# Where the first layer's modulation is multiplied: TensorE rows in quarters of the array, or sums on VectorE

## The chip, the cores and the metric

The kernel runs on one core of a Trainium2 chip. The metric is the device time of one execution in microseconds (us), the median of several runs. The engines are TensorE (PE in the profile, its weight loads PEld), VectorE (DVE), ScalarE (ACT), GpSimd (POOL) and SyncE (SP), whose queue issues nearly all transfers here.

## The reference

A trunk of two layers over 512 tokens of 1024 features, all in float32. A vector `c` gives each layer six modulation vectors; here is what matters of the first layer.

```python
c_act = jax.nn.silu(c)
shift1, scale1, gate1, shift2, scale2, gate2 = jnp.split(c_act @ ada_w[l] + ada_b[l], 6, axis=-1)
h = modulate(rms_norm(x, norm1_g[l]), shift1, scale1)          # h * (1 + scale) + shift
mix = s5_mixer(h, ...)                                         # state space per group of 16 channels, then gelu(y) * sigmoid(gelu(y) @ w_glu + b_glu)
x = x + gate1[:, None, :] * mix
h = modulate(rms_norm(x, norm2_g[l]), shift2, scale2)
x = x + gate2[:, None, :] * swiglu(h, ffn_w_gate[l], ffn_w_up[l], ffn_w_down[l])
```

`c_act @ ada_w[0]` is one row times a matrix of 1024 x 6144, 25.2 MB of weights that are read once. The second layer is attention with shared keys and values and a feed-forward of the same kind, and has its own six vectors, besides two for the keys.

## The kernel before

Features lie on the 128 partitions, in eight tiles of 128; `self.mod` holds all modulation vectors as columns, eight for each vector of 1024. The stages follow one another: the mixer (`s5`), its GLU (`glu`), the feed-forward of layer 0 (`ffn`), attention (`mla`), the feed-forward of layer 1. A scheduler orders the instructions of each engine from the order in which the program is written and from its own estimate of when each is ready; `issue_after` holds an instruction behind another one of the same engine. Each engine, and SP's queue, then runs its list in order. Large products take float32 weights as a high and a low part: `wsplit` loads a raw tile of 512 KB on SP (ring of three buffers, tag `raw`), ScalarE rounds it (L790), GpSimd subtracts (L150), and TensorE makes three passes (L801 to L803). In the GLU and the feed-forward, work is due by a clock of the products traced so far (`tick`, `later`, `chain`).

Layer 0's modulation comes in three ways. Shift1 and scale1 are row products (`ada_row`, L380 to L383): the weights stream through TensorE, the stationary operand is `c_act` repeated over all 128 columns, and four PSUM banks (tag `ad`) hold the result on all partitions; VectorE picks each channel with a mask `sel` and a sum (L628, L629). Gate1 is a job of `ada_jobs` in the mixer: SP loads eight blocks of 128 x 1024 (L274), VectorE multiplies each by a scalar for each partition and adds it to `acc` (L282, L284), and the partitions are summed at the end (L292, L296, L318). Shift2 and scale2 are two such jobs, spread over the GLU's products, one step for each 1.5 us of the clock, with the partition sum as products with ones (L305). Gate2 is the first two of 18 jobs of 128 x 512 blocks that are spread over the feed-forward, one of 144 steps for each 1.8 us of the clock; the other sixteen serve keys and layer 1.

In the mixer, `x` is loaded (L392), turned and squared; the sum of squares (L431) gives the norm of each token. The loop over `q` builds the input and output maps on VectorE, GpSimd and TensorE (L579). `sgu` is the input modulation for each group, and `u` the modulated input (L641, L649). `kernels(q)` makes products on TensorE (L612), adds the skip on VectorE (L147), writes to DRAM (`kd`, L618) and reads the windows back (`tt`, L620); `sums` and `states` make the chunk states (L679, L693), `intra` and `inter` the outputs (L721, L732).

The GLU's first half of the tokens ends in a norm (`norm`, L849, L857), whose result the feed-forward's first products need; the second half's products are made meanwhile.

## Time and profile before

| | us |
|---|---|
| median of 3 runs | 1350.58 |
| lowest and highest | 1349.37, 1353.07 |
| span of the profiled execution, first to last instruction | 1353.7 |
| first product of the GLU (L801) | 193.44 |
| first sum for the norm behind the GLU (L849) | 254.93 |
| last step of the modulation on VectorE (L284) | 686.36 |

The only time recorded for the profiled execution is its span. A row of the timeline gives the start in us from the span's start, the duration, the engine, the line, the operation, its output and inputs by name with partitions x elements, and in brackets the idle time before it with what ended it. One float32 product shows as two records on TensorE.

### The profile page before, as it was taken

How to read it: one execution, taken by the hardware profiler on the slowest of the kernel's cores; microseconds unless marked ns; L12 is line 12 of the kernel's file. 1: busy time of each engine (PE TensorE's matmuls, PEld its weight loads, DVE VectorE, ACT ScalarE, POOL GpSimd, SP SyncE). 2: the span in 40 equal slices, each digit the busy share in tenths (PEclk: the TensorE clock that was granted, in tenths of full speed). 3: DMA queues.
4: the chain of work that ended last, by engine and by line, in shares of the span. 5: the costliest groups of instructions: out<-in, count | busy, mean ns of one | idle time of the engine just before them, and what ended most of it. 6: DMA issues, size and time to landing. Idle time of an engine off the chain costs nothing.

```text
span 1353.7 us, 17703 instructions
## 1 busy us (share of the span) xinstructions
PE 1178.7 (87%) x6649; PEld 989.5 (73%) x6649; DVE 861.0 (64%) x1328; ACT 494.9 (37%) x921; POOL 623.8 (46%) x369
## 2 busy tenths in 40 slices
PE   6727669789998899969599788999899999999998
PEld 3416558688776677758499677888898888888888
DVE  8898989978666777766677899895942222221000
ACT  3314363334112121222236786784432222222222
POOL 6984834625333444443372434414724444444445
PEclk8858889789998999979699899999999999999999
DMA  8503977525556666465564011102522333333333
GB/s 206 156 16 59 107 234 222 171 79 158 174 170 191 185 200 190 145 183 167 176 184 130 28 32 47 32 17 75 165 73 84 94 97 97 96 91 94 104 110 110
DMA packets 230293, 167.46 MB, mean 124 GB/s; under 512 B 10000, under 2 KB 204480, under 8 KB 230208
## 3 DMA queue, kind: packets, MB, share of 16 engines
q1 hardware_dynamic: 229888, 166.31, 43.6%
q8 instruction: 52, 0.85, 0.3%
q14 instruction: 33, 0.27, 0.1%
q10 hardware_dynamic: 320, 0.02, 0.0%
HBM read 163.23 MB, written 3.08 MB: 123 GB/s over the span
## 4 chain that ended last, share of the span: by engine, by line
PE 42%; DVE 32%; DMA 17%; ACT 4%; issue 4%; SPq 0%; POOL 0%; ACTq 0%; DVEq 0%; POOLq 0%
PE ps L801 12%; PE ps L802 12%; PE ps L803 12%; DMA a<-in_ada_w 10%; DVE a L284 9%; DMA a<-in_kv_ada_w 4%; DVE a L144 3%; DVE sums L147 2%; DVE a L809 2%; DVE a L282 2%; DVE a L150 2%; DMA a<-in_x 1%; PE ad L382 1%; PE ps L132 1%; DVE xT L881 1%
## 5 line engine op out<-in xcount | busy, mean ns | idle before, releaser
L150 POOL TENSOR_TENSOR wl<-raw,wh 128x1024 fp32r<-128x1024 f32 (+1 forms) x179 | 435.0, 2438 | 542.9 <-ACT wh L790 497.4
L803 PE MATMUL ps<-a,wl 128*128 128x512 f32 (+1 forms) x1406 | 502.9, 359 | 18.5 <-POOL wl L150 18.5
L801 PE MATMUL ps<-a,wh 128*128 128x512 f32 (+1 forms) x1406 | 499.2, 359 | 12.9 <-DMA a<-in_ada_w 6.0
L802 PE MATMUL ps<-a,wh 128*128 128x512 f32 (+1 forms) x1406 | 501.0, 358 | 9.7 <-DVE a L809 5.3
L803 PEld LDWEIGHTS ps<-a,wl 128*128 128x128 f32 x1406 | 271.4, 194 | 64.4 <-POOL wl L150 24.3
L801 PEld LDWEIGHTS ps<-a,wh 128*128 128x128 f32 x1406 | 269.0, 193 | 55.9 <-ACT wh L790 7.0
L802 PEld LDWEIGHTS ps<-a,wh 128*128 128x128 f32 x1406 | 271.2, 193 | 51.2 <-DVE a L809 5.8
L790 ACT CAST wh<-raw 128x1024 fp32r<-128x1024 f32 (+1 forms) x179 | 181.5, 1018 | 337.4 <-PE ps L802 173.6
L284 DVE SCALAR_TENSOR_TENSOR a<-a,csil,a 128x512 f32<-128x512 f32 (+1 forms) x140 | 186.7, 1334 | 99.5 <-DMA a<-in_ada_w 71.2
L999 DVE TENSOR_TENSOR si<-si,ps 128x512 f32<-128x512 f32 x44 | 30.1, 684 | 154.2 <-PE ps L803 143.2
L808 ACT CAST a<-si 128x512 fp32r<-128x512 f32 x44 | 27.3, 621 | 204.8 <-DVE si L999 204.8
L881 DVE SCALAR_TENSOR_TENSOR xT<-ps,mod,xT 128x256 f32<-128x256 f32 (+1 forms) x35 | 20.2, 577 | 128.1 <-PE ps L803 128.1
L809 DVE TENSOR_TENSOR a<-si,a 128x512 fp32r<-128x512 f32 x44 | 70.7, 1609 | 21.5 <-ACT a L808 21.5
L132 PE MATMUL ps<-ident,a 128*128 128x128 f32 (+1 forms) x304 | 45.1, 288 | 20.6 <-DVE a L1338 6.2
L132 PEld LDWEIGHTS ps<-ident,a 128*128 128x128 f32 (+1 forms) x304 | 36.3, 141 | 27.1 <-issue 6.6
L147 DVE TENSOR_TENSOR sums<-sums,sq 128x256 f32<-128x256 f32 (+1 forms) x36 | 43.9, 1219 | 12.0 <-ACT sq L834 11.5
L834 ACT ACTIVATE sq<-xT 128x256 f32<-128x256 f32 (+1 forms) x36 | 16.3, 452 | 74.5 <-DVE xT L881 71.2
L144 POOL TENSOR_TENSOR ro<-a,rt 128x256 f32<-128x256 f32 (+2 forms) x24 | 13.6, 589 | 60.2 <-ACT a L1351 45.3
L579 PE MATMUL ps<-ident,a 128*128 128x128 f32 x64 | 12.9, 355 | 32.1 <-DVE a L150 32.1
L1412 ACT ACTIVATE a<-ps,mn 128x128 f32<-128x128 f32 (+1 forms) x64 | 34.4, 546 | 16.0 <-DVE mn L1411 15.9
L382 PE MATMUL ad<-adaw,csil 128*128 128x512 f32 x64 | 36.9, 717 | 0.9 <-DMA adaw<-in_ada_w 0.9
L802 PE MATMUL ps<-a,a 128*128 128x256 f32 (+2 forms) x108 | 34.9, 324 | 3.1 <-DVE a L809 3.1
(314 smaller groups left out, 1730.8 us busy)
## 6 DMA issues: line engine op xcount, KB each, us to landing
a<-in_ada_w SPq DMA_DIRECT2D x112, 256.0 KB, 2.9
raw<-in_ffn_w_gate SPq DMA_DIRECT2D x44, 512.0 KB, 4.1
raw<-in_ffn_w_up SPq DMA_DIRECT2D x44, 512.0 KB, 3.9
raw<-in_ffn_w_down SPq DMA_DIRECT2D x42, 512.0 KB, 4.0
adaw<-in_ada_w SPq DMA_DIRECT2D x24, 512.0 KB, 4.6
a<-in_ada_w SPq DMA_DIRECT2D x16, 512.0 KB, 4.8
a<-in_kv_ada_w SPq DMA_DIRECT2D x32, 256.0 KB, 3.5
raw<-in_ffn_w_down SPq DMA_DIRECT2D x21, 384.0 KB, 3.8
```

The lines of the kernel that those rows point to most:

```text
L132: self.nc.tensor.transpose(out=out, in_=in_, identity=ident)
L144: return eng.tensor_tensor(out=out, in0=a, in1=b, op=ALU.mult)
L147: eng.tensor_tensor(out=out, in0=a, in1=b, op=ALU.add)
L150: eng.tensor_tensor(out=out, in0=a, in1=b, op=ALU.subtract)
L284: v.scalar_tensor_tensor(out=acc, in0=x, scalar=self.csil[:, k:k + 1], in1=acc, op0=ALU.mult, op1=ALU.add)
L382: nc.tensor.matmul(pr[i * 2 + h], lhsT=self.csil[:, k:k + 1].to_broadcast([P, P]), rhs=w[:, h * 512:(h + 1) * 512], start=(k == 0), stop=( ...
L790: nc.scalar.copy(out=flat(wh), in_=flat(raw))
L801: mm(out, lhsT=lhs[0], rhs=rhs[0], start=start, stop=False)
L802: mm(out, lhsT=lhs[0], rhs=rhs[1], start=False, stop=False)
L803: self.last_mm = mm(out, lhsT=lhs[1], rhs=rhs[0], start=False, stop=stop).ins
L809: self.nc.vector.tensor_tensor(out=lo, in0=src, in1=hi.bitcast(F32), op=ALU.subtract)
L1412: nc.scalar.activation(out=p[:, self.OFF[t]:self.OFF[t] + w], in_=pt, func=AF.Exp, scale=-1.0, bias=mn[:, t:t + 1], accum_out=su[:, t:t + 1])
```

## The change

All six vectors of layer 0 become row products on TensorE inside the mixer. A step of the new `ada_rows` takes two of the eight row blocks: two loads of 512 KB, then four products of 512 columns. Each has `c_act` over 32 columns only and writes one quarter of the partitions of a single PSUM bank (`ac`): two quarters for each row block, one for each half of its columns. After four such pairs a closing step copies the bank to SBUF on ScalarE and adds the quarters in pairs while it turns the row to columns (four products with `self.rows`); VectorE adds the bias. There are four buffers: three of the ring `raw` and one of its own. The steps (six times four pairs and a closing) are placed by hand: five before the loop over `q`, one in each of its eight turns, five behind `states(0)`, five behind `kernels(3)`, two behind each `inter(q)`. `vectors` moves ahead of them. `sgu` is now made from columns of `self.mod` by products with a mask `spread`. The VectorE jobs for gate1, shift2, scale2 and gate2 go, with the tail for `direct`; PSUM gives one bank of `ad` to `ac`, and `intra` runs three instead of four ahead.

```diff
@@ -68,17 +67,17 @@
         self.psum = None
-        self.banks(ps=2, pb=2, ad=4)
+        self.banks(ps=2, pb=2, ad=3, ac=1)
         self.xT = self.const.tile([P, KT, S], F32, tag="xT", name="xT")
@@ -234,8 +233,11 @@
+        self.rows = self.cst([P, 2], name="rows")
+        nc.vector.tensor_tensor(out=self.rows, in0=self.ident[:, 0:64:32], in1=self.ident[:, 64:128:32], op=ALU.add)
     def vectors(self, pool):
@@ -258,14 +260,45 @@
-    def ada_jobs(self, jobs, w, new, ahead=3, direct=False):
+    def ada_rows(self, jobs, pool):
+        nc, v = self.nc, self.nc.vector
+        def pair(src, col0, i):
+            if i == 0:
+                self.rows_acc = self.ps("ac")
+            ks = (2 * i, 2 * i + 1)
+            ws = [self.ring.tile([P, 1024], F32, tag="raw", name=self.name("adaw"), bufs=3) if k % 4 < 3 else
+                  pool.tile([P, 1024], F32, tag="adaw", name=self.name("adaw")) for k in ks]
+            for k, w in zip(ks, ws):
+                nc.sync.dma_start(out=w, in_=src[k * P:(k + 1) * P, col0:col0 + 1024])
+            for j in range(4):
+                nc.tensor.matmul(self.rows_acc[32 * j:32 * j + 32], lhsT=self.csil[:, ks[j // 2]:ks[j // 2] + 1].to_broadcast([P, 32]),
+                                 rhs=ws[j // 2][:, j % 2 * 512:j % 2 * 512 + 512], start=(i == 0), stop=(i == 3))
+        def close(at):
+            row = self.tmp.tile([P, 512], F32, tag="t1", name=self.name("adrow"))
+            nc.scalar.copy(out=row, in_=self.rows_acc)
+            pt = self.ps()[:, 0:8]
+            for m in range(4):
+                nc.tensor.matmul(pt[:, 2 * m:2 * m + 2], lhsT=row[:, m * P:(m + 1) * P], rhs=self.rows, start=True, stop=True)
+            cols = lambda t: t[:, at:at + 8].rearrange("a (h m) -> a m h", h=2)
+            v.tensor_tensor(out=cols(self.mod), in0=pt.rearrange("a (m h) -> a m h", h=2), in1=cols(self.adab), op=ALU.add)
+        for src, col0, at in jobs:
+            for i in range(4):
+                yield lambda src=src, col0=col0, i=i: pair(src, col0, i)
+            yield lambda at=at: close(at)
+    def ada_jobs(self, jobs, w, new, ahead=3):
...
-        def end(at, acc):
-            pt = self.ps("st")[:, 0:8]
-            with self.tc.issue_after(self.last_mm):
-                for m in range(8):
-                    nc.tensor.matmul(pt[:, m:m + 1], lhsT=acc[:, m * P:(m + 1) * P], rhs=self.ones[:, 0:1], start=True, stop=True)
-            self.add(v, self.mod[:, at:at + 8], pt, self.adab[:, at:at + 8])
         def flush():
-            while whole:
-                end(*whole.pop(0))
             if not ends:
@@ -372,28 +393,17 @@
-            pr = [self.ps("ad") for _ in range(4)]
-            def ada_row(k, i):
-                w = self.ring.tile([P, 1024], F32, tag="raw", name=self.name("adaw"), bufs=3)
-                load = nc.sync.dma_start(out=w, in_=io["ada_w"][0, k * P:(k + 1) * P, i * 1024:(i + 1) * 1024])
-                for h in range(2):
-                    nc.tensor.matmul(pr[i * 2 + h], lhsT=self.csil[:, k:k + 1].to_broadcast([P, P]), rhs=w[:, h * 512:(h + 1) * 512],
-                                     start=(k == 0), stop=(k == KT - 1))
-                return load
-            for n in range(3):
-                ada_row(n // 2, n % 2)
             xj = self.at(X0, [P, 8, 512])
...
                 nc.sync.dma_start(out=xj[h * 64:(h + 1) * 64], in_=xv[h])
-                ada_row((3 + h) // 2, (3 + h) % 2)
             craw = self.at(V0, [P, 2, 2, 4, 64])
...
                 nc.sync.dma_start(out=craw[:, i], in_=io[key].rearrange("o (b t a) p n -> (o a p) b t n", b=2, t=4))
+            self.vectors(sp)
+            ada = self.ada_rows(ada, sp)
+            step = lambda n=1: [f() for f in itertools.islice(ada, n)]
             v.tensor_copy(out=lam[64:96].rearrange("a (b n) -> a b n", b=2),
@@ -521,29 +531,13 @@
             self.add(v, b_s, b_r, b_i)
-            self.acc = sp.tile([P, 1024], F32, tag="acc", name="acc")
...
-            sel = sp.tile([P, 16], F32, tag="sel", name="sel")
-            nc.vector.tensor_reduce(out=sel, in_=self.ident.rearrange("a (r p) -> a p r", p=16), axis=AX.X, op=ALU.add)
             bd = [self.at(M0 + 4 * i, [P, 32, 32]) for i in range(2)]
@@ -554,9 +548,8 @@
             self.mul(g, dsk, dcol.unsqueeze(2).to_broadcast([32, 32, 16]), eye.unsqueeze(1).to_broadcast([32, 32, 16]))
-            for n in range(5, 12):
-                ada_row(n // 2, n % 2)
+            step(5)
             ww = [self.at(W0 + 8 * q, [P, 2, 8, P]) for q in range(4)]
@@ -580,8 +573,7 @@
                 with tc.issue_after(done.ins):
-                    if q % 2 == 0:
-                        row = ada_row(6 + q // 4, q // 2 % 2)
+                    step()
                 with tc.issue_after(copied.ins):
@@ -620,19 +612,20 @@
+            spread = self.at(U0, [P, 8, 8, 16])
+            nc.scalar.copy(out=spread, in_=self.ident.rearrange("a (l p) -> a l p", p=16).unsqueeze(2).to_broadcast([P, 8, 8, 16]))
+            mc = sp.tile([P, 2, 8], F32, tag="mc", name="mc")
+            v.tensor_copy(out=mc[:, 0], in_=self.mod[:, 0:8])
+            v.scalar_tensor_tensor(out=mc[:, 1], in0=self.mod[:, 8:16], scalar=1.0, in1=self.n1g[:, 0:8], op0=ALU.add, op1=ALU.mult)
+            px = self.ps()
+            for l in range(8):
+                nc.tensor.matmul(px[:, l * 16:(l + 1) * 16], lhsT=spread[:, l].rearrange("a r p -> a (r p)"),
+                                 rhs=mc.rearrange("a s f -> a (s f)"), start=True, stop=True)
             sgu = sp.tile([P, 2, 32, 2], F32, tag="sgu", name="sgu")
             for i in range(2):
-                for h in range(2):
-                    big = self.at(U0 + 8 + h * 2, [P, 32, 16])
-                    self.mul(v, big, pr[2 * i + h].rearrange("a (g p) -> a g p", p=16), sel.unsqueeze(1).to_broadcast([P, 32, 16]))
-                    v.tensor_reduce(out=sgu[:, i, :, h], in_=big, axis=AX.X, op=ALU.add)
-            f3 = lambda t: t.rearrange("a g b -> a (g b)")
-            self.add(v, f3(sgu[:, 0]), f3(sgu[:, 0]), f3(vec[:, 0]))
-            self.add(v, f3(sgu[:, 1]), f3(sgu[:, 1]), f3(vec[:, 1]))
-            v.scalar_tensor_tensor(out=f3(sgu[:, 1]), in0=f3(sgu[:, 1]), scalar=1.0, in1=f3(vec[:, 2]), op0=ALU.add, op1=ALU.mult)
-            for _ in range(3):
-                next(ada)()
+                v.tensor_copy(out=sgu[:, i].rearrange("a (f l) b -> a l b f", l=8),
+                              in_=px[:, 0:P].rearrange("a (l s b f) -> a l s b f", l=8, s=2, b=2)[:, :, i])
             kernels(0)
@@ -752,36 +745,29 @@
             states(0)
-            gate = sums(2)
+            step(5)
+            sums(2)
             kernels(2)
...
             kernels(3)
-            with tc.issue_after(row.ins):
-                self.vectors(sp)
-            with tc.issue_after(gate.ins):
-                for _ in range(EARLY):
-                    next(ada)()
+            step(5)
             intra(2)
-            intra(3)
             for q in range(8):
                 inter(q)
-                if q < 4:
-                    intra(q + 4)
+                if q < 5:
+                    intra(q + 3)
                 if q in (1, 3):
                     states(q // 2 + 2)
-                if q == 3:
-                    with tc.issue_after(self.s5_last.ins):
-                        for _ in range(KT - EARLY):
-                            next(ada)()
+                step(2)
+            step(99)
             self.dump("u", u)
...
             self.dump("gel", gel)
-            return next(ada)
     def wsplit(self, shape, src, dst=None):
@@ -919,7 +905,7 @@
-    def glu(self, between, extra):
+    def glu(self, between):
...
-        rest = self.spread_out(extra, 0.5, 1.5, lambda: (self.last_raw,))
-        def after(h):
-            if h == 0:
-                rest()
-            between(h)
...
-        self.outputs(blocks, lambda k: (hi[k], lo[k]), done, 6, after)
+        self.outputs(blocks, lambda k: (hi[k], lo[k]), done, 6, between)
@@ -1455,21 +1434,18 @@
         a0, a1, kv = io["ada_w"][0], io["ada_w"][1], io["kv_ada_w"]
-        first, then = [(a0, 16 * P, 16, 8)], [(a0, at * P, at, 8) for at in (24, 32)]
-        later = [(a0, at * P, at, 4) for at in (40, 44)] + [(kv, 4 * i * P, 96 + 4 * i, 4) for i in range(4)]
+        first = [(a0, at * P, at) for at in (0, 8, 16, 24, 32, 40)]
+        later = [(kv, 4 * i * P, 96 + 4 * i, 4) for i in range(4)]
         later += [(a1, 4 * i * P, 48 + 4 * i, 4) for i in range(12)]
-        end = self.s5(self.ada_jobs(first, lambda n: self.ring.tile([P, n * P], F32, tag="raw", name=self.name("adaw"), bufs=3),
-                              lambda n: self.acc))
+        self.s5(first)
         self.banks(ps=6, st=2)
         self.wring = self.ctx.enter_context(self.tc.tile_pool(name="wring", bufs=4, reuse_waits="tile"))
-        buf, acc = itertools.cycle((80, 84, 88)), itertools.cycle((92, 76))
-        end()
-        self.glu(self.ffn_in(0), self.ada_jobs(then, lambda n: self.at(next(buf), [P, n * P]), lambda n: self.at(next(acc), [P, n * P]), direct=True))
+        self.glu(self.ffn_in(0))
         self.dump("x1", self.xT)
```

## Rows read from the trace of the kernel before

**Rows 1.** The page's chain that ended last: shares of the span by engine.
```profile
PE 42%; DVE 32%; DMA 17%; ACT 4%; issue 4%; SPq 0%; POOL 0%; ACTq 0%; DVEq 0%; POOLq 0%
```

**Rows 2.** Busy time by stretch: us, busy by engine, granted clock, transfers' share, GB/s.
```profile
0.00:49.00 49.00, 36.61 (x153) 21.04 (x153) 40.06 (x135) 16.90 (x46) 35.71 (x76) 0.93 0.79 208
...
109.00:153.00 44.00, 32.45 (x444) 29.72 (x446) 40.10 (x43) 18.18 (x48) 31.21 (x18) 0.84 0.59 77
153.00:193.00 40.00, 27.84 (x250) 25.06 (x245) 33.45 (x39) 18.45 (x37) 18.27 (x9) 0.87 0.79 163
193.00:255.00 62.00, 49.84 (x313) 45.31 (x312) 59.78 (x53) 25.06 (x42) 34.32 (x13) 0.85 0.76 231
...
315.00:432.00 117.00, 109.23 (x460) 85.26 (x459) 80.92 (x108) 24.28 (x32) 44.10 (x17) 0.96 0.59 176
432.00:570.00 138.00, 126.47 (x538) 97.36 (x537) 100.03 (x97) 32.22 (x44) 55.77 (x21) 0.96 0.62 187
570.00:687.00 117.00, 89.13 (x438) 73.12 (x437) 80.06 (x74) 26.39 (x34) 46.67 (x21) 0.85 0.59 174
```

**Rows 3.** The chain in order of time, 0 to 260 us: start, us, what.
```profile
7.17 16.39 DMA a<-in_x
...
254.93 0.87 PE st L849 x4
```

**Rows 4.** VectorE's waits, 0 to 108 us: us in total, times, longest.
```profile
DVE var L210 <- PE ps L431: 6.2, 1, 6.2
```

**Rows 5.** Timeline of the mixer: start us, us, instruction.
```profile
73.17 13.78 DVE L144 TENSOR_TENSOR a<-a,pw 128x512 f32<-128x512 f32 x1
74.17 9.79 POOL L150 TENSOR_TENSOR a<-a 128x512 f32<-128x512 f32 x8
...
100.80 0.68 DVE L144 TENSOR_TENSOR a<-ad,sel 128x512 f32<-128x512 f32 x1
...
108.48 0.22 DVE L633 SCALAR_TENSOR_TENSOR sgu<-sgu,vec 128x64 f32<-128x64 f32 x1
```

**Rows 6.** Timeline of the mixer, weight loads of row, half and whole-array products.
```profile
15.41 0.19 PEld L382 LDWEIGHTS ad<-adaw,csil 128*128 128x128 f32 x1 [0.24 <-issue]
15.84 0.19 PEld L382 LDWEIGHTS ad<-adaw,csil 128*128 128x128 f32 x1 [0.24 <-issue]
...
165.33 0.85 PEld L721 LDWEIGHTS ad<-a,a 128*64 128x64 f32 x16 [0.17 <-issue]
...
178.31 3.07 PEld L732 LDWEIGHTS ad<-a,a 128*128 128x128 f32 x26
```

**Rows 7.** Transfers by line: count, KB of one, median us from issue to landing.
```profile
adaw<-in_ada_w SPq DMA_DIRECT2D x24, 512.0 KB, 4.6
...
kd<-a SPq DMA_DIRECT2D x4, 240.0 KB, 7.8
```

**Rows 8.** Waits of SP's own queue, 100 to 200 us.
```profile
SPq L618 <- DVE a L147: 28.1, 4, 12.9
```

**Rows 9.** VectorE's waits, 108 to 193 us.
```profile
DVE acc L284 <- DMA adaw<-in_ada_w: 6.1, 1, 6.1
```

**Rows 10.** Groups by line, 193 to 255 us: busy us, mean ns; idle before.
```profile
L150 POOL TENSOR_TENSOR wl<-raw,wh 128x1024 fp32r<-128x1024 f32 x11 | 30.7, 2796 | 23.0 <-ACT wh L790 20.1 <-PE st L305 2.9
L284 DVE SCALAR_TENSOR_TENSOR a<-a,csil,a 128x1024 f32<-128x1024 f32 x14 | 26.1, 1866 | 0.9 <-DMA a<-in_ada_w 0.8
L801 PE MATMUL ps<-a,wh 128*128 128x256 f32 x73 | 22.0, 301 | 1.4 <-ACT wh L790 1.4
...
L802 PE MATMUL ps<-a,a 128*128 128x512 f32 x16 | 7.5, 468 | 3.1 <-DVE a L809 3.1
```

**Rows 11.** Timeline of the feed-forward, the first and last of a run of products.
```profile
400.04 0.39 PE L801 MATMUL ps<-a,wh 128*128 128x512 f32 x1
...
406.11 0.39 PE L803 MATMUL ps<-a,wl 128*128 128x512 f32 x1
```

**Rows 12.** TensorE's waits, 305 to 700 us.
```profile
PE st L318 <- DVE part L296: 16.5, 1, 16.5
```

More of the change, by code (lines that the diff above doesn't have):

```diff
@@ L40 @@
 ARENA = 128
-EARLY = 4
 class Scratch:
@@ L259, in vectors @@
         self.kvag, self.qg = cols[:, 48:50], cols[:, 50:52]
-    def ada_jobs(self, jobs, w, new, ahead=3, direct=False):
+    def ada_rows(self, jobs, pool):
[24 more added lines that the diff above has]
+    def ada_jobs(self, jobs, w, new, ahead=3):
         nc, v = self.nc, self.nc.vector
         loads = [(src[k * P:(k + 1) * P, col0:col0 + n * P], n) for src, col0, at, n in jobs for k in range(KT)]
-        tiles, ends, whole = [], [], []
+        tiles, ends = [], []
         def load():
@@ L285, in product @@
             load()
-            if k == KT - 1 and direct:
-                whole.append((at, acc))
-                self.later(3.0, flush)
-            elif k == KT - 1:
+            if k == KT - 1:
                 for a in range(0, n, 4):
```

12 lines of the change are left out of this document (removed).

## The prediction

> **What bounds the kernel now.** I read the page first: of the span, 1353.7 us, TensorE has the largest share of the chain that ended last (42%), VectorE follows with 32%, and waiting for transfers is 17% [rows 1]. That is a mean over stages with different limits, so the second view is the busy time by stage [rows 2]. The reader is to see three kinds of stage there. In the mixer (up to about 193 us) VectorE is busy 40.1 of 44 and 33.5 of 40 us. In the GLU (193 to 255 us) VectorE is busy 59.8 of 62 us while TensorE has idle time. In the first feed-forward TensorE leads, but not fully: 109.2 of 117, 126.5 of 138 and 89.1 of 117 us. After 687 us no instruction of layer 0's modulation is left. So only these three stages can change, and each is costed by what ends its waits last.
>
> **The change part by part.**
>
> *Start of the mixer, up to its input modulation.* Four row loads of 512 KB stand before the end of x's two loads on SP's queue, and x ends a wait of 16.39 us on the chain [rows 3]. VectorE sits idle 6.2 us for the sum of squares of x (L431) [rows 4]. The change puts the row loads behind x: 2.1 MB less ahead of it, at 208 GB/s [rows 2] 10 us of transfer. So that idle gap closes: 6.2 us. The eight small loads of `vectors` move here too, behind x on the same queue; nothing early needs them. The extraction of shift and scale takes VectorE from 100.80 to 108.70 us [rows 5], 7.9 us; its replacement is one ScalarE copy of 128x1024 (twice the 0.68 us of the 128x512 row: 1.4), eight products of 16 columns (at most sixteen records of 0.118 us [rows 6], 1.9; I take 1.0) and two copies to 128x64 (0.22 us each [rows 5]), an estimate of 3 us. That gives 4.9 us, together 11.1. I take 9, because this stretch is also ruled by collisions of VectorE and GpSimd: one 128x512 multiply took 13.78 us while GpSimd did eight subtractions [rows 5], and another order of the same work can collide worse. Ends: 3 and 14.
>
> *The row products themselves.* Before, a product of 512 columns is two records, 0.43 us apart [rows 6]; a pair of loads would be four products, eight records, 3.44 us one after another. In the new form each product fills 32 columns of the array and writes 32 partitions of one PSUM bank. The nearest rows are products that fill halves: their weight loads are 0.85/16 = 0.053 us apart, against 3.07/26 = 0.118 us for whole-array products of as many columns [rows 6]. Halves of one bank thus overlap fully. For quarters the bounds are 3.44 us (no overlap) and 0.86 us (four at once); I take 1.0 us, near the row of the halves. At the change of form stands an idle time of 0.17 us [rows 6], two for each pair, so a pair costs TensorE 1.34 us; 24 pairs cost 32 us. Before the second half of the mixer they fall in a stretch where TensorE waits for VectorE. In 109 to 193 us TensorE idles 44 - 32.5 + 40 - 27.8 = 23.7 us [rows 2], and the eleven pairs that are traced from there on need 14.7. Without that idle time they would cost those 14.7 us. The six closings (a ScalarE copy of 128x512, four small products, an addition) lie on ScalarE's idle time, which is busy 18.2 of 44 and 18.5 of 40 us [rows 2]; uncovered, at 0.68 us a copy, they would cost 4 us. The one accumulator bank makes the next job's first pair wait for the copy, which the loads ahead of it hide.
> The Trainium skill (TensorEngine Tiling (Array Packing), Tiling Modes, Key Properties) says that a change of tiling mode drains the engine. It gives no figure; the idle time just named is what the trace has for it, and without it eleven pairs would need 11 us instead of 14.7, which leaves the sum as it is.
>
> *Second half of the mixer.* Removed: eight VectorE steps of 128x1024 and their tail, and VectorE's wait of 6.1 us for such a load [rows 9]. With five steps behind that wait, at 1.87 us as in the GLU [rows 10], that would be 15 us if VectorE alone set this stretch. But the end hangs on the chain kernels, write to DRAM, read back, products inside a chunk, and on this chain SP waits 28.1 us for VectorE's addition [rows 8], and the write takes 7.8 us to land [rows 7]. Moved here: the loads of 16 steps of 512 KB from the GLU and 16 of 256 KB from the feed-forward, 12.6 MB, all on SP's queue, some of them now ahead of or behind those DRAM round trips, and ahead of the first GLU weights, which use the same three buffers. The mixer's 24 row loads become 48. About 18 of them are left for this stretch after those already in flight, ten more than the eight before. Where transfers were dense they moved 208 GB/s at 0.79 and 231 GB/s at 0.76 of the engines' time [rows 2], 263 to 304 at full share, so 512 KB take 1.7 to 2.0 us and ten such loads 17 to 20 us, where transfers idle 44 x 0.41 + 40 x 0.21 = 26 us [rows 2]. They barely fit. TensorE takes its queue in order: where a pair's load is late, state sums and output products queue behind it, VectorE waits for those, and GpSimd for VectorE. I take a loss of 3 us; ends: a loss of 18 (the ten loads unhidden, at the middle price) and a gain of 15.
>
> *GLU.* Sixteen steps leave VectorE: 14 of L284 alone are 26.1 us busy [rows 10] of its 59.8, and two first ones (L282) go as well, besides 16 matmuls for the partition sums. The norm of the first token half, whose first products (L849) run at 254.93 us [rows 3], no longer waits for VectorE. What is late next? TensorE has run 218 records of 256 columns and 48 of 512 by then; at 0.117 and 0.2335 us (26 records in 6.07 us [rows 11], half of it for half the columns) that is 36.7 us, of which about 9 (some 75 records of 256 columns) belong to the second half already. GpSimd's weight splits take 2.8 us each [rows 10], eight of them 22 us. So the norm could start at about 193 + 28 us, and with an allowance of 10 us for the split of the first inputs and the last tile's additions at 231 us instead of 254.9: 23 us at most (an estimate). Some of that is given back: the products of the second half still have to run behind it, and each needs a GpSimd split that blocks VectorE's additions. I take 18; ends 9 and 23.
> The Trainium skill (SBUF — State Buffer, Who interferes with whom) says that a VectorE instruction with two SBUF inputs and a GpSimd one that reads SBUF exclude each other for a whole instruction. The 13.78 us row agrees. By that rule the VectorE instructions that stay are still blocked, which is the third rival below.
>
> *First feed-forward.* Its chain of steps loses the first 16 of 144 (gate2). Between 315 and 687 us TensorE is idle 7.8 + 11.5 + 27.9 = 47.2 us [rows 2], in part a single wait of 16.5 us for the last steps [rows 12]. Per step that is 0.33 us, so 16 steps are 5.2 us; I take 6. Ends: 2 (the waits are those for weight splits) and 14 (nearly the whole late wait goes).
>
> **Sum.** 9 - 3 + 18 + 6 = 30 us off the profiled span: 1353.7 - 30 = 1323.7. The profiled execution's span is 3.1 us over the median of the runs shown, 1350.58, so I forecast 1321 us (1320.6).
>
> **The rivals.**
> *Slower: row loads hold TensorE in the second half of the mixer.* A row load takes 4.6 us to land [rows 7]. If SP issues each of the eleven pairs only when TensorE already waits, because SP itself sits behind a DRAM round trip [rows 8], the exposed time is 11 x 4.6 = 50.6 us. Against the other gains, 9 + 18 + 6 = 33, the kernel is 17.6 us slower: 1368 us. It decides from 3 us exposed per pair on. For it: one queue, in order, with 28.1 us of blocked issue. Against: four buffers, so two pairs are fetched ahead. 0.10; a milder form that gives back just the gains and ends near 1350: 0.05.
> *Quarters do not overlap.* Then the change does not do what it says: a pair is 3.44 + 0.34 = 3.78 us, eleven are 42 us, 18 over the idle time, and the time is 1339 us. The halves speak against it. 0.10.
> The Trainium skill (TensorEngine Tiling (Array Packing), Gotcha 1: PSUM Pressure) says that row tiles can't use one PSUM bank at once; carried over to these column quarters, which share a bank, it gives this rival. The halves [rows 6] also share one bank and overlap, so the trace speaks against that reading.
> *GpSimd's splits become the GLU's limit.* With 2.8 us per split, and VectorE's additions blocked behind them, the GLU gains 7 instead of 18: 1332 us. For it: GpSimd is busy 34.3 of those 62 us already. 0.12.
> *The second half of the mixer gains.* If the loads fit, VectorE's 6.1 us wait and its steps give 10 there instead of costing 3: 1308 us. 0.18.
>
> **How the numbers follow.** The forecast has 0.40, with its own range 1311 to 1332; gains beyond all of these have 0.05. A measurement of this kernel tells changes from about 0.3% on, 4 us. Faster: 0.40 + 0.10 + 0.12 + 0.18 + 0.05 = 0.85; within: 0.05; slower: 0.10. The range 1302 to 1345 holds the forecast and the last three rivals, 0.80.
>
> **What would show it.** Right: the first product of the GLU lies within some 15 us of 193 us; no VectorE instruction with the modulation's weights lies before the feed-forward; the four weight loads of a pair start well under 0.43 us apart; L849's first products come some 20 us earlier relative to the GLU's start; the feed-forward's steps number 128. Wrong: TensorE shows long waits for `adaw` or `raw` loads between its state sums, or SP a larger wait at the DRAM round trip; or VectorE is as busy in the GLU as before, behind GpSimd. What would make the prediction wrong altogether is a mixer that ends over 30 us later.

## The result, and the profile after

The changed kernel takes 1336.54 us (median; 1332.93 to 1340.58), the kernel before 1349.97 on the same chip: ratio 0.9888, 95% interval 0.9855 to 0.9921. It is faster by 13.4 us. The profiled executions differ by 17.3 us (1353.7 and 1336.4). The table cuts both traces at the same marks: the end of the copy or addition that completes `sgu`, SP's issue of the fourth kernel write (`kd`), the first product of the GLU, the first products of the two norms behind it, and the last residual addition of the first feed-forward. Gains are taken before rounding.

| stretch of the profiled execution, us | before | after | gained | predicted |
|---|---|---|---|---|
| start to `sgu` | 108.7 | 101.8 | 6.9 | 9 (3 to 14) |
| `sgu` to the fourth kernel write | 44.7 | 73.1 | -28.4 | -3 (-18 to 15) for this and the next |
| fourth kernel write to the GLU's first product | 40.0 | 40.2 | -0.2 | |
| GLU's first product to the norm of the first half | 61.4 | 43.0 | 18.3 | 18 (9 to 23) |
| norm of the first half to that of the second | 34.7 | 38.1 | -3.4 | 6 (2 to 14) for this and the next |
| to the last residual of the feed-forward | 436.5 | 415.9 | 20.6 | |
| the rest | 627.7 | 624.2 | 3.5 | 0 |

The busy times by stretch, as in [rows 2], of the changed kernel; the fourth row is the GLU's stretch by its own marks, and the second fence has the same stretch of the kernel before:

```profile
0.00:49.00 49.00, 21.61 (x143) 12.54 (x143) 24.89 (x119) 16.57 (x44) 15.80 (x49) 0.97 0.74 196
109.00:153.00 44.00, 28.28 (x355) 21.42 (x353) 36.42 (x39) 11.86 (x28) 41.44 (x25) 0.84 0.55 122
153.00:193.00 40.00, 27.86 (x248) 21.99 (x244) 24.71 (x23) 13.70 (x24) 20.53 (x12) 0.87 1.01 176
215.16:258.19 43.03, 37.63 (x254) 34.71 (x254) 30.84 (x26) 23.53 (x37) 32.75 (x14) 0.96 0.53 154
570.00:687.00 117.00, 107.12 (x569) 91.47 (x570) 68.91 (x67) 34.09 (x46) 63.76 (x28) 0.94 0.58 171
```

```profile
193.44:254.79 61.35, 49.19 (x310) 44.69 (x308) 59.34 (x52) 24.41 (x41) 33.88 (x13) 0.85 0.76 231
```

In the GLU's stretch VectorE was busy 59.3 of 61.4 us and is busy 30.8 of 43.0; TensorE was busy 49.2 of 61.4 and is busy 37.6 of 43.0, now the largest share. VectorE no longer sets this stretch, as predicted. From 570 to 687 us TensorE is busy 107.1 us against 89.1. The rows of the mixer tell the other story. In the first 49 us GpSimd is busy 15.8 us instead of 35.7, VectorE 24.9 instead of 40.1; GpSimd's work turns up after 109 us (41.4 instead of 31.2). From 153 to 193 us transfers are busy all the time.

Why the start is empty, from TensorE's and GpSimd's timelines of the changed kernel (start, us, instruction, in brackets the idle time before it and what ended it), and in the third fence the same two instructions before:

```profile
20.71 0.35 PE L255 MATMUL ps<-ident,rows_a 52*128 52x52 f32 x1 [18.16 <-DMA rows_b<-in_ada_b]
20.99 0.42 PE L410 MATMUL ps<-ident,a 96*128 96x96 f32 x1
```
```profile
30.29 0.24 POOL L143 TENSOR_TENSOR r<-a 128x32 f32<-128x32 f32 x1 [26.82 <-DVE a L146]
```
```profile
3.91 0.42 PE L400 MATMUL ps<-ident,a 96*128 96x96 f32 x1 [1.32 <-DVE a L397]
12.30 0.24 POOL L144 TENSOR_TENSOR r<-a 128x32 f32<-128x32 f32 x1 [8.87 <-DVE a L147]
```

The transpose L255 belongs to `vectors`. It stands ahead of the transpose of the state matrix (L410; L400 before), which ran at 3.9 us before, and waits 18.2 us for the small loads, which stand behind x on SP's queue. VectorE's discretisation waits for L410, and GpSimd, which takes it up, starts at 30.3 us instead of 12.3.

SP's queue in the second half (start, us of issue, what, how many):

```profile
97.90 8.09 SPq L275 DMA_DIRECT2D adaw<-in_ada_w  x4
128.49 0.34 SPq L610 DMA_DIRECT2D kd<-a  x1
131.03 4.03 SPq L612 DMA_DIRECT2D tt<-kd  x8
...
174.93 0.30 SPq L610 DMA_DIRECT2D kd<-a  x1
...
177.57 3.74 SPq L612 DMA_DIRECT2D a<-kd  x8
181.43 23.38 SPq L275 DMA_DIRECT2D adaw<-in_ada_w  x11
208.56 4.22 SPq L774 DMA_DIRECT2D raw<-in_s_w_glu  x3
```

Between 106 and 128 us SP issues nothing: it waits for the addition that completes the first kernel (22.5 us), and the row loads behind the write wait with it. The fourth write comes at 174.9 us. Then eleven row loads take 23.4 us, 2.1 us each, and only behind them come the GLU's weights. TensorE, which takes its queue in order too:

```profile
129.73 1.87 PE L285 MATMUL ps<-rows,adrow 128*128 128x2 f32 x8 [11.68 <-ACT adrow L282]
...
161.32 1.98 PE L714 MATMUL ad<-a,a 128*64 128x128 f32 x16 [7.31 <-DMA adaw<-in_ada_w]
...
193.57 1.05 PE L277 MATMUL ac<-adaw,csil 128*32 128x512 f32 x4
...
196.09 1.05 PE L277 MATMUL ac<-adaw,csil 128*32 128x512 f32 x4
...
211.32 1.06 PE L277 MATMUL ac<-adaw,csil 128*32 128x512 f32 x8
...
215.16 0.47 PE L787 MATMUL ps<-a,a 128*128 128x512 f32 x1 [0.36 <-DVE mod L287]
```

It stands 11.7 us for the closing's copy on ScalarE, which is queued behind work that waits for VectorE, and 7.3 us for a row load ahead of products (L714) that need none. The rows of L277 are row products. A pair has eight records (four products of two records each), as in the row at 211.32 us: 1.06 us. The two rows of four records are half pairs, the products of one load. Each half took 1.05 us too, so a pair whose loads come apart, as most of these late ones do, takes TensorE about twice the time.

### The profile page after: what moved, and what is told of

It is laid out like the page before. It is cut to its first block, busy times and chain, and to the rows that moved or that the text cites. A ratio compares the mean times of both kernels' runs of the same rounds, so it can differ in the third digit from the quotient of the medians.

```text
span 1336.4 us, 17897 instructions
## 1 busy us (share of the span) xinstructions
PE 1173.5 (88%) x6790; PEld 987.6 (74%) x6790; DVE 781.0 (58%) x1275; ACT 498.3 (37%) x924; POOL 624.8 (47%) x369
## 4 chain that ended last, share of the span: by engine, by line
PE 47%; DVE 27%; DMA 16%; ACT 4%; issue 3%; SPq 2%; POOL 0%; DVEq 0%; ACTq 0%; POOLq 0%
PE ps L788 12%; PE ps L787 12%; PE ps L789 12%; DMA a<-in_ada_w 8%; DVE a L317 6%; DMA a<-in_kv_ada_w 3%; DVE sums L146 3%; DVE a L795 2%; DVE a L143 2%; DMA adaw<-in_ada_w 2%; DVE a L149 2%; PE ps L131 1%; PE ac L277 1%; PE ad L725 1%; DVE a L861 1%
## 5 line engine op out<-in xcount | busy, mean ns | idle before, releaser
L789 PE MATMUL ps<-a,wl 128*128 128x512 f32 (+1 forms) x1406 | 498.5, 356 | 17.2 <-POOL wl L149 17.2
L787 PE MATMUL ps<-a,wh 128*128 128x512 f32 (+1 forms) x1406 | 494.3, 355 | 12.3 <-ACT wh L776 9.6
L787 PEld LDWEIGHTS ps<-a,wh 128*128 128x128 f32 x1406 | 269.9, 194 | 49.7 <-ACT wh L776 11.7
L776 ACT CAST wh<-raw 128x1024 fp32r<-128x1024 f32 (+1 forms) x179 | 181.8, 1018 | 322.7 <-PE ps L788 174.8
L317 DVE SCALAR_TENSOR_TENSOR a<-a,csil,a 128x512 f32<-128x512 f32 x112 | 139.1, 1242 | 91.2 <-DMA a<-in_ada_w 68.2
L795 DVE TENSOR_TENSOR a<-si,a 128x512 fp32r<-128x512 f32 x44 | 77.1, 1754 | 21.6 <-ACT a L794 21.6
L146 DVE TENSOR_TENSOR sums<-sums,sq 128x256 f32<-128x256 f32 (+1 forms) x36 | 51.6, 1434 | 14.5 <-ACT sq L820 14.1
L277 PE MATMUL ac<-adaw,csil 128*32 128x512 f32 x192 | 40.9, 737 | 5.2 <-DMA adaw<-in_ada_w 5.2
L149 POOL TENSOR_TENSOR a<-raw,a 128x1024 fp32r<-128x1024 f32 (+1 forms) x8 | 19.1, 2399 | 56.0 <-DMA raw<-in_s_w_glu 40.0
L572 PE MATMUL ps<-ident,a 128*128 128x128 f32 x64 | 13.4, 355 | 27.0 <-DVE a L149 22.1
L572 PEld LDWEIGHTS ps<-ident,a 128*128 128x128 f32 x64 | 9.4, 182 | 37.1 <-issue 20.0
```

Source lines behind the costliest of these rows:

```text
L146: eng.tensor_tensor(out=out, in0=a, in1=b, op=ALU.add)
L149: eng.tensor_tensor(out=out, in0=a, in1=b, op=ALU.subtract)
L277: nc.tensor.matmul(self.rows_acc[32 * j:32 * j + 32], lhsT=self.csil[:, ks[j // 2]:ks[j // 2] + 1].to_broadcast([P, 32]), rhs=ws[j // 2][: ...
L317: v.scalar_tensor_tensor(out=acc, in0=x, scalar=self.csil[:, k:k + 1], in1=acc, op0=ALU.mult, op1=ALU.add)
L776: nc.scalar.copy(out=flat(wh), in_=flat(raw))
L787: mm(out, lhsT=lhs[0], rhs=rhs[0], start=start, stop=False)
```

## The experiments

Every ratio is to runs of the kernel before on the same chip; as its median was between 1349.07 and 1356.21 us from one group of runs to the next, the ratios are compared, not the times. All marks are from the profiled executions, in us. "Late vectors" is the kernel of experiment 1, and "early" is the loop over `q`. Experiments 2, 4, 8 and the first of 9 leave part of the modulation out and set `self.mod` to zero with one instruction on GpSimd, which the cuts below leave out.

| kernel | ratio (95%) | `sgu` | 1st write | 4th write | GLU's first product | first norm |
|---|---|---|---|---|---|---|
| before | 1 | 108.7 | 117.2 | 153.4 | 193.4 | 254.8 |
| changed | 0.9888 (0.9855, 0.9921) | 101.8 | 128.5 | 174.9 | 215.2 | 258.2 |
| late vectors | 0.9811 (0.9776, 0.9845) | 87.6 | 115.0 | 161.8 | 203.7 | 248.4 |
| changed, two jobs | 0.9705 (0.9660, 0.9750) | 98.0 | 123.4 | 167.0 | 192.9 | 234.2 |
| changed, no loads | 0.9748 (0.9711, 0.9786) | 100.3 | 126.0 | 169.8 | 199.3 | 242.9 |
| before, no gate | 0.9861 (0.9828, 0.9894) | 108.0 | 116.5 | 152.7 | 192.0 | 252.2 |
| late vectors, maps first | 0.9815 (0.9785, 0.9845) | 89.7 | 119.8 | 156.4 | 205.8 | 251.9 |
| late vectors, 12 steps early | 0.9671 (0.9631, 0.9711) | 85.0 | 101.4 | 149.7 | 185.5 | 230.8 |
| changed, one group | 0.9925 (0.9898, 0.9953) | 105.9 | 112.8 | 145.2 | 223.3 | 264.1 |
| late vectors, 16 steps early | 0.9612 (0.9572, 0.9651) | 92.3 | 100.0 | 139.8 | 181.8 | 225.4 |
| before, no late steps | 0.9802 (0.9765, 0.9838) | 107.7 | 116.2 | 152.4 | 195.6 | 237.9 |
| late vectors, two jobs | 0.9560 (0.9527, 0.9593) | 86.1 | 110.1 | 152.5 | 176.0 | 217.7 |
| 16 steps early, two jobs first | 0.9753 (0.9721, 0.9784) | 115.9 | 112.0 | 151.2 | 194.7 | 238.4 |
| late vectors, kernel first | 0.9733 (0.9695, 0.9772) | 83.0 | 97.5 | 133.0 | 197.1 | 241.8 |

**1. Late vectors.**

```diff
-            self.vectors(sp)                    # right behind x
...
+            self.vectors(sp)
             step(5)
```

> The changed kernel, with the small vector loads and their two transposes put behind the discretisation instead of right behind x. Three theories for the mixer's second half, which took 114 us from the modulation's copy (sgu) to the GLU's first product, against 85 us before. A, late start: TensorE's 18.2 us wait for the small loads (rows_b) at the start delays the discretisation, with it GpSimd's output maps (GpSimd starts at 30.3 us instead of 12.3), and these delay the first kernel write (128.5 us instead of 117.2) and all behind it; then this kernel gets back the start and most of the second half: GLU's first product at 190 to 200 us instead of 215, time 1313 to 1322. B, row loads: SP's queue and the transfers of the moved rows set the second half; then the start is won and mostly lost again there: first product at 207 to 215, time 1329 to 1337. C, TensorE and ScalarE: the row products and their closings set it; the same as B here.

The transpose of the state matrix is back at 3.9 us, GpSimd starts at 12.3, `sgu` is complete at 87.6. SP issues the small loads as early as in the changed kernel (9.97 to 19.5 us); what has moved is their transposes on TensorE. So the place of these transposes had cost 14 us at the start. But the first write comes 27 us behind `sgu`, as in the changed kernel, and the GLU starts at 203.7, between what A and B expected; the ratio (0.981, 1323.52 us) is between them too. Late vectors are a part of the loss, not its whole.

**2. Changed, two jobs.**

```diff
-        first = [(a0, at * P, at) for at in (0, 8, 16, 24, 32, 40)]
+        first = [(a0, at * P, at) for at in (0, 8)]
```

> The changed kernel with only the first two jobs (shift and scale of the mixer) multiplied; the other four jobs (32 row loads, their products and closings) are left out, their modulation is zero. A, late start: the second half keeps most of its length, over 100 us from sgu to the GLU's first product, and the time stays above 1322. B or C (the moved work itself): that stretch falls back to 85 to 90 us and the time to 1307 to 1313. The difference to the changed kernel is the whole price of the moved rows in the second half.

From `sgu` to the GLU 94.9 us instead of 113.3: the moved rows cost 18.5 us there, 4.1 of them ahead of the fourth write and 14.4 behind it. Yet `sgu` to the fourth write stays 69.0 us, where the kernel before needs 44.7. Most of the 28.4 us lost in that part does not come from the row work. The time, 1310.95, is what B and C expected; the first part is what A expected, so neither is enough.

**3. Changed, no loads.** For the last four jobs:

```diff
-            for k, w in zip(ks, ws):
-                nc.sync.dma_start(out=w, in_=src[...])
+            if col0 < 2048:                     # as before
+                ...
+            else:
+                ws = [self.xT[:, 0:2].rearrange("a k s -> a (k s)")] * 2
```

> The changed kernel with the row loads of the last four jobs left out: their products read tiles that lie on the chip already, so products, closings and additions stay and 16.8 MB of transfers go; the modulation is wrong. B, row loads: most of the loss goes, sgu to the GLU's first product 85 to 95 us, time 1307 to 1316. C, products and closings: it stays above 105 us, time above 1328. A: above 100 us, time above 1322.

99.0 us from `sgu` to the GLU: of the 18.5 us, 14.3 are the loads' and 4.2 the products' and closings'. C falls as the main cause; B holds for the tail (29.5 us instead of 40.2 behind the fourth write), not ahead of it (69.5).

**4. Before, no gate.**

```diff
-        later = [(a0, at * P, at, 4) for at in (40, 44)] + [(kv, ...
+        later = [(kv, ...
```

> The kernel before, with the first 16 of the 144 steps in the first feed-forward (the gate of that layer) left out; that gate is zero. The prediction gave these steps 6 us (0.33 us of TensorE's idle time for each): then the time is 1343 to 1346. Rival: TensorE's 16.5 us wait for the last steps' sum goes wholly, as the changed kernel's stage, shorter by some 21 us, suggests: 1327 to 1335.

18.3 us, the rival. TensorE's wait of 16.5 us for the last steps' sum [rows 12] is gone, and the stretch behind 570 us, in which the granted clock was 0.85 [rows 2], runs at 0.96:

```profile
PE st L319 <- DVE part L297: 0.6, 1, 0.6
```
```profile
570.00:700.00 130.00, 119.38 (x722) 104.31 (x721) 80.50 (x96) 43.94 (x65) 71.47 (x31) 0.96 0.56 166
```

The last step ends at 634.6 us instead of 689.1: sixteen steps are 54.5 us of that chain, 3.4 us each, and before it reached past the products that were to cover it. The prediction had divided idle time by steps; but this was one wait at the end of the chain, and with sixteen steps fewer nearly all of it goes.

**5. Late vectors, maps first.** On top of the first experiment, `mapped` being GpSimd's last correction of the output maps:

```diff
+                with tc.issue_after(mapped.ins):   # states(q): multiplications and, for q < 2, the memset
```

> The kernel of the first experiment (late vectors), with GpSimd made to finish all its output maps before it clears the state tiles and turns the first chunk states; nothing else is changed. In the changed kernel and in the first experiment the modulation's copy to the first kernel write takes 27 us (before: 8.5), whatever row work follows, and GpSimd's last corrections of the output maps lie between its state multiplications. Theory D, the order: GpSimd's maps come too late for the kernels, because the order of its queue puts state work ahead of them; then the fourth kernel write moves from 161.8 us to 150 to 156, the GLU's first product from 203.7 to 192 to 198, and the time falls from 1323.5 to 1312 to 1319. Rival, the amount: GpSimd and VectorE have the same work either way and only swap which is late; the time stays within 3 us of 1323.5.

The fourth write comes 5.4 us earlier, but the first 4.8 later and the GLU 2.1 later; the ratio does not move. D falls in this form: GpSimd's own order is not what holds the first kernel.

**6. Late vectors, 12 and 16 steps early.** In the loop over the input maps:

```diff
                 with tc.issue_after(done.ins):
-                    step()
+                    step(2 if q % 2 else 1)        # 16 steps: step(2)
```

> The kernel of the first experiment, with 12 instead of 8 steps of the row products in the loop over the input maps, so that four fewer (three or four pairs, 1 MB each) are left for the second half, where twelve row loads stood between the last map read and the GLU's first weights (25 us of issue). If the row loads set that tail (the fourth kernel write to the GLU's first product: 42 us here, 26 without the moved jobs, 30 without their loads), it falls by 6 to 10 us and the time to 1313 to 1318; if TensorE's wait for early rows holds up the maps, the copy of the modulation moves later by as much and the time stays at 1320 to 1326.

> As the kernel with 12 steps in the loop over the input maps, with 16 steps there (two for each of its eight rounds). If the row loads set the tail before the GLU, another 5 to 8 us are won, 1306 to 1312; if the loop then waits for rows (transfers were busy a third of the time there, 112 GB/s), the copy of the modulation moves from 87.6 to over 95 us and the time is that of 12 steps or more.

Both beat the forecasts: 0.967 and 0.961 (1310.31 and 1302.0 us, beside 1355.1 of the kernel before). With 12 steps the tail is 35.8 us, 6 shorter as expected. But the larger part came unasked: the first write is at 101.4 and 100.0 us, 16 and 8 us behind `sgu` instead of 27. With 16 steps the tail is 42.0 us again: the fourth write comes 9.9 us earlier than with 12, the GLU's first product 3.7. SP's queue with 16 steps:

```profile
42.32 54.04 SPq L275 DMA_DIRECT2D adaw<-in_ada_w  x26
100.02 0.34 SPq L610 DMA_DIRECT2D kd<-a  x1
...
139.81 0.33 SPq L610 DMA_DIRECT2D kd<-a  x1
...
148.49 1.27 SPq L275 DMA_DIRECT2D adaw<-in_ada_w  x2
...
161.61 28.44 SPq L774 DMA_DIRECT2D raw<-in_s_w_glu  x8
```

The last row loads now leave at 148.5 us, ahead of the reads of the fourth kernel, and none stands between them and the weights of the GLU. Two things have changed at once here, the number of row loads left and the order that the scheduler chose; experiment 10 takes them apart.

**7. Changed, one group.** In 18 of 24 pairs:

```diff
-                nc.tensor.matmul(self.rows_acc[32 * j:32 * j + 32], ...
+                o = 32 * j if i == 3 else 0
+                nc.tensor.matmul(self.rows_acc[o:o + 32], ...
```

> The changed kernel, with the four products of a pair in one quarter of the array and one group of 32 partitions, one after another, in 18 of the 24 pairs; the modulation is wrong. If the four quarters work at once (a pair of 1.05 us instead of about 3.4), TensorE's row products take some 40 us more here; if that work is hidden in TensorE's waits, as the prediction had it, the time is 1336 to 1342; if it is on the path from the modulation to the GLU, 1345 to 1365. If the quarters do not work at once, a pair takes as long as before and the time is that of the changed kernel, 1336.

TensorE's timeline at a steady clock, two pairs in one group and one pair in four quarters:

```profile
60.67 3.62 PE L278 MATMUL ac<-adaw,csil 128*32 128x512 f32 x8
...
65.25 3.62 PE L278 MATMUL ac<-adaw,csil 128*32 128x512 f32 x8
...
69.82 1.06 PE L278 MATMUL ac<-adaw,csil 128*32 128x512 f32 x8
```

3.62 us against 1.06: the quarters do work at once, 3.4 times as fast. The Trainium skill (TensorE: Matmul & The Clock Gate, Measured speedup vs the span model) gives 2.38 for three column tiles and 3.07 for four row tiles; four column tiles here are above both. The time grows by 0.4% only, about 5 us for some 46 us more of TensorE's work (18 times 2.56), and the intervals overlap. But that does not show the work to be hidden: the scheduler chose another order here, with the first write at 112.8 us and the fourth at 145.2, 29.7 us earlier than in the changed kernel. From there to the GLU's first product it takes 78.1 us instead of 40.2, with TensorE busy for 74.3 of them:

```profile
145.18:223.26 78.08, 74.26 (x493) 40.29 (x494) 34.95 (x40) 24.81 (x47) 24.52 (x14) 0.95 0.76 196
```

So the longer pairs are on the path here, and the better order ahead of them covers most of their price.

**8. Before, no late steps.**

```diff
-        first, then = ..., [(a0, at * P, at, 8) for at in (24, 32)]
+        first, then = ..., []                     # and the gate's steps left out, as in 4
```

> The kernel before, with the steps that the change moves out of the GLU and the first feed-forward left out altogether (16 and 16; that part of the modulation is zero). The mixer is untouched, so this gives the GLU's and the feed-forward's terms without what the moved work costs in the mixer. The feed-forward's 16 steps alone gave 18 us. If the GLU's steps are worth the 18 us of the prediction (9 to 23), the ratio to the kernel before is 0.969 to 0.978, 1307 to 1320 us at a time before of 1349; if the GLU is bound by GpSimd's weight splits and gains 7 as the rival had it, 0.980 to 0.984.

The GLU's stretch falls from 61.4 to 42.3 us, the 18 of the prediction and a little more. Yet the ratio is 0.980, what the rival expected and only 0.6 points below that without the gate's steps, and the intervals overlap. The rest is lost elsewhere: the GLU's first product comes 3.6 us later than there, and from the second norm to the last residual it takes 425.0 us against 413.8. The granted clock of TensorE shows where, in three stretches of this kernel and, in the second fence, the same stretches behind the norm of the one without the gate's steps:

```profile
370.00:410.00 40.00, 35.38 (x144) 27.40 (x144) 26.16 (x24) 6.79 (x9) 15.01 (x6) 0.91 0.57 172
410.00:500.00 90.00, 77.26 (x313) 59.34 (x312) 63.74 (x63) 21.10 (x28) 34.60 (x13) 0.92 0.62 182
500.00:600.00 100.00, 84.21 (x344) 64.67 (x344) 69.39 (x63) 21.05 (x28) 40.62 (x17) 0.91 0.58 169
```

```profile
383.00:423.00 40.00, 34.52 (x144) 26.63 (x145) 26.77 (x30) 7.99 (x12) 13.62 (x7) 0.96 0.59 180
423.00:513.00 90.00, 82.72 (x352) 63.34 (x351) 65.21 (x64) 19.10 (x26) 37.39 (x14) 0.98 0.62 190
513.00:613.00 100.00, 82.91 (x348) 63.87 (x347) 66.33 (x62) 22.21 (x29) 39.96 (x16) 0.91 0.56 171
```

0.91, 0.92, 0.91 against 0.96, 0.98, 0.91: lower in the first two. What lowered it there is not settled. A gain that shows in its own stage can thus lose some 11 us in a later one.

**9. Without the late rows, and too many early ones.** The first experiment with two jobs only; and 16 steps early with `step(10)` in place of `step(5)` ahead of the loop.

> The kernel of the first experiment (late vectors) with only the first two jobs multiplied; the row work of the other four is left out, their modulation is zero. Two things are open about the changed kernel's second half: whether the 27 us from the modulation's copy to the first kernel write come from the row work, and what the row work costs with the start mended. If the 27 us are GpSimd's maps and the order around them, they stay above 20 here, the fourth kernel write comes at 150 to 156 us (153.4 before) and the GLU's first product at 176 to 184; ratio 0.958 to 0.965. If they are the row work, the first kernel write follows within 12 us, the GLU starts at 160 to 170, ratio under 0.955.

> As the kernel with 16 steps in the loop over the input maps, and ten steps (two jobs) ahead of that loop instead of five, so that four of the 30 steps are left for the second half. If late row loads still cost there, the ratio falls from 0.961 to 0.954 to 0.959; if the transfers are now too dense ahead of the loop, the modulation's copy moves later than 92.3 us and the ratio is 0.960 to 0.968.

Without the late rows, but with the start mended, the first write still comes 24 us behind `sgu`, at 110.1, and the fourth at 152.5, where the kernel before has it. So nearly all of the 27 us is not the work of the moved rows. The kernel with 16 steps early, which does all of the work, is only 0.5 points above this one; this is no lower limit, though, for the kernel without the late rows still has the order of experiment 1. With two jobs ahead of the loop `sgu` slips to 115.9 and the ratio rises from 0.961 to 0.975: 32 row loads in a row take SP 69.3 us, TensorE waits 9.1 us for rows, and the maps' transposes behind them wait 8.1 us for a closing.

**10. Late vectors, kernel first.** On top of the first experiment, `kadd` being VectorE's addition to the first kernel:

```diff
-            sums(0)
+            with tc.issue_after(self.kadd.ins):
+                sums(0)
```

> The kernel of the first experiment (late vectors), with the first chunk sums ordered behind VectorE's addition to the first kernel, and nothing else changed: the row work, its eight steps in the loop and its loads stay. It tells the order of the queues apart from the amount of row work. In the first experiment GpSimd has the first output map ready at 93 us, but TensorE's kernel products run at 102 to 106 (behind the first two chunk sums), ScalarE's copies at 107.5 (behind one that waits for a scan), the addition at 113.6, and SP's queue, with row loads behind the write, stands still for 21.7 us until 115.0. Theory E, order: the first write moves from 115.0 to 98 to 104 us, the fourth from 161.8 to 140 to 150, the row loads behind them come earlier, the GLU starts at 184 to 194 instead of 203.7; ratio 0.962 to 0.972. Rival, amount: the writes come earlier, but the row loads and VectorE's scans, now behind the kernels, keep the GLU at 199 or later; ratio 0.977 to 0.984, as in the first experiment (0.981).

The addition is what the first write waits for; holding VectorE's part of the first chunk sums behind it lets the kernel go first. In the first experiment, TensorE's first kernel products (L604) stand behind the second chunk sums (L672, the row of 64), and a closing behind them waits for ScalarE. In the kernel before, in the second fence, the kernel products (L612) are first and those sums (L679) behind them:

```profile
99.81 2.35 PE L672 MATMUL ps<-a,a 128*64 128x64 f32 x64 [1.63 <-DVE m L143]
102.09 3.68 PE L604 MATMUL pb<-a,a 128*32 128x128 f32 x32
118.53 1.87 PE L285 MATMUL ps<-rows,adrow 128*128 128x2 f32 x8 [12.75 <-ACT adrow L282]
```

```profile
111.83 3.68 PE L612 MATMUL pb<-a,a 128*32 128x128 f32 x32
...
120.40 2.08 PE L679 MATMUL ps<-a,a 128*64 128x64 f32 x64
```

The SP queue of the first experiment, and below it that of this one:

```profile
84.08 9.15 SPq L275 DMA_DIRECT2D adaw<-in_ada_w  x3
114.98 0.34 SPq L610 DMA_DIRECT2D kd<-a  x1
...
161.84 0.30 SPq L610 DMA_DIRECT2D kd<-a  x1
...
169.22 25.10 SPq L275 DMA_DIRECT2D adaw<-in_ada_w  x12
198.27 11.67 SPq L774 DMA_DIRECT2D raw<-in_s_w_glu  x5
```

```profile
97.50 0.34 SPq L610 DMA_DIRECT2D kd<-a  x1
...
107.99 0.31 SPq L610 DMA_DIRECT2D kd<-a  x1
...
119.75 13.56 SPq L610 DMA_DIRECT2D kd<-a  x2
...
157.23 30.39 SPq L275 DMA_DIRECT2D adaw<-in_ada_w  x14
191.58 13.42 SPq L775 DMA_DIRECT2D raw<-in_s_w_glu  x6
```

With one constraint on the order the first write moves from 115.0 to 97.5 us and the fourth from 161.8 to 133.0, earlier than E expected. But the GLU starts only 6.6 us earlier, at 197.1, and the ratio, 0.9733, lies between E's 0.972 and the rival's 0.977: fourteen row loads, 30.4 us, now stand where twelve stood. Both causes are real and lie one behind the other: mend the order, and the row loads on the one queue are the next bound; thin out these as well (experiment 6), and both gains come through.

## Why the prediction was right, and where its sizes were off

The time, 1336.5 us, is in the range (1302 to 1345) and the direction is right; it is 15.5 us above the forecast and 4.5 above the forecast's own range. It is in the range partly by luck: the second half of the mixer loses 25.6 us more than forecast, and the first feed-forward, which gains 11.2 us more, covers less than half of that. Of the prediction's own signs, the GLU's norm came 18.3 us earlier from the GLU's start ("some 20") and 128 steps are left in the feed-forward, but the GLU's first product comes 21.7 us later ("within some 15 us"), TensorE waits 7.3 us for a row load, and SP's longest wait at a kernel write grew from 12.9 to 22.5 us, both named as signs of being wrong.

- **Start of the mixer: 9, measured 6.9, for other reasons.** SP's queue had three row loads ahead of x, not four (the next is issued at 16.96 us, behind the matrix C); they are gone from there, as said. But the 6.2 us were not won here: x's first transposes, at 23.7 us before, come at 25.5 us in the changed kernel and only in experiment 1 at 17.0. The step that failed is "nothing early needs them" of the eight small loads: nothing needs their data, but TensorE takes its list in order, and their transposes stood ahead of the state matrix. Experiment 1 prices it: `sgu` 14.2 us earlier. Without it the term would have been 21 us, above its upper end of 14.
- **Row products: a pair 1.34, measured 1.06 us when both loads are there, and about 2.1 when they come apart.** No idle time of TensorE shows at the two changes of form. That quarters in one bank overlap is shown by experiment 7; that the work is hidden is not: in the changed kernel products and closings cost 4.2 us (experiment 3). Thirteen pairs, not eleven, fall behind the loop.
- **Second half of the mixer: a loss of 3, measured 28.6.** This is the term that failed, outside its own bounds. The loads cost 14.3 us, somewhat less than the "17 to 20 us" of an unhidden transfer, and behind the fourth write the kernel loses only 0.2 us, because they take the place of VectorE's steps. What it lacked is the 24 us ahead of the fourth write. The scheduler now puts the first two chunk sums ahead of the first kernel on TensorE, ScalarE and VectorE; SP, with row loads behind the write, stands still. Experiments 2 and 9 show that the moved rows are not needed for it, 10 that a change of the order alone undoes it, on the kernel of experiment 1.
- **The slower rival** (row loads hold TensorE) had the mechanism right and the size too large: 14.3 us over thirteen pairs are 1.1 us for each, not 4.6, and below the 3 us at which it decides.
- **GLU: 18, measured 18.3**, and 19.0 in experiment 8. The rival in which GpSimd's splits bind falls.
- **First feed-forward: 6, measured 17.2** (20.6 less 3.4 between the norms). Experiment 4 finds 18.3 for the sixteen steps alone. Both lie above the term's upper end of 14, "nearly the whole late wait goes", which was the case.

By the measured terms: 6.9 - 28.6 + 18.3 + 17.2 + 3.5 = 17.3 us between the profiled executions.

What stays open: what the scheduler's estimate turned on when it changed the order (in experiments 6 and 7 it chose the good order unasked), the clock in experiment 8, and what the changed kernel would gain by the order alone, with its small vectors still at the start. The Trainium skill (DMA: Bandwidth & Descriptors, Issuing engines are not separate DMA queues) says that starting transfers from several engines saves only the time to start them. Here SP's issue of a row load takes 0.4 us, but its waits in order held the loads for 22.5 us at a stretch; whether another engine's queue would free them was not tried.

## What to carry to other kernels

Work that comes off a bound engine early in a stage is worth only as much as the next thing in line is ready for: look up what that is, and whether a scheduler will now order the queues differently. When transposes, copies or loads that "nobody needs yet" move, look at what stands behind them on their engine; in order, they hold it all. Spread streamed loads over the stretch where the queue is idle, and keep them from standing behind a write that waits for another engine: the version with 16 steps early and late vectors, 0.9612 of the kernel before, does the same work as the changed kernel at 0.9888.

## What the runs showed of the hardware

Four products that each fill a quarter of the columns of TensorE's array and write one quarter of a PSUM bank's partitions ran at once, 1.06 us instead of 3.62 when all four went to one quarter (experiment 7). Two such products in two quarters took 1.05 us, as long as the four. In the changed kernel SP took 5.88 us to issue the second of the two loads of the output matrix C and 6.66 us for the next two small loads, while x was in transfer; the small loads behind them took 0.25 to 0.37 us each.
